# In the second block's mixer, the delta rule's steps and the taps of its q and v are traced ahead of the linear attention's

## The chip, the cores and the metric

The kernel runs on one core of one Trainium2 chip. The core has a matrix engine (PE, whose weight loads are listed apart as PEld), a vector engine (DVE), an activation engine (ACT), GpSimd (POOL), and a queue engine (SP) that issues the loads from memory. Each engine takes its instructions in a fixed order, one after the other, and an instruction starts when the work it depends on is done. The metric is the device time of one execution in microseconds (us).

## What is computed

Two transformer blocks of 256 tokens, one after the other; each has a sequence mixer and a feed-forward part. The change touches the second block's mixer of the 256 "latent" tokens. It multiplies the normalized tokens by one weight matrix of 1024 x 4624 and splits the product into the inputs of two mixers of four heads with 128 channels each, whose outputs are gated, normalized by head, put side by side and multiplied by an output matrix. Of the reference:

```python
def gla_chunk_scan(q, k, v, log_f, s0):        # the linear attention ("hg")
    '''S_t = diag(f_t) S_{t-1} + k_t v_t^T, o_t = S_t^T q_t.'''

def gated_delta_chunk_scan(q, k, v, beta, log_a, s0):   # the delta rule ("dn")
    '''S_t = a_t (I - beta_t k_t k_t^T) S_{t-1} + beta_t k_t v_t^T, o_t = S_t^T q_t.'''
    ...
    sol = lax.linalg.triangular_solve(a_mat, rhs, left_side=True, lower=True, unit_diagonal=True)

def gated_head_norm(o, gate, w):
    y = rms_norm_2(o, w) * jax.nn.silu(gate)

def hybrid_mixer_2(pc, px, lb, hg_norm_w, conv_w, a_log, dt_bias, dn_norm_w):
    ...
    return jnp.concatenate([hg_c, dn_c], axis=-1), jnp.concatenate([hg_x, dn_x], axis=-1)
```

Both recurrences run in both directions. The delta rule's q, k and v go through a 3 x 3 convolution first. After the mixer come the output projection with its residual, a router, and 16 experts.

## The kernel before

**The mixer of the latents** (`mixer2`, L1585 to L1631) is a row of projections with side work between them. For every 1 MB tile of weights, `wtile` (L260) starts a load, `split_to` (L242) makes the high part of it on ACT (a CAST) and the low part on DVE (`whl`, L243), and three products of high and low parts go to the PE (L223, tile `b`). After every tile, `pump` (L200) steps the side work: a list of Python generators, `side`, of which it takes the first, steps it once, and puts it at the back; one that returns "idle" (it waits for data that is not there yet) is passed over. `rate` says how many steps a tile gets, 5 at first and 6 later. `drain` steps on until the list is empty.

**The side generators** are:
- `dn_conv` (L1254): a projection of the delta rule (k, then q, then v), and a generator `taps` with the eight shifted products of the convolution on DVE (`qkv`, L1282).
- `dn_core` (L1318): the delta rule for two blocks of 128 tokens in two directions. The triangular inverse is built up in levels: on the PE `qp` and `dy`, on ACT a copy `Q` (L1429), on DVE a masked copy into `Y` (L1436) and transposes `T` (L1418). Then come the attention matrices (`qk`, `rb`, `att`), the weights `wT`, and four steps one after the other (`vn`, `qs`, `dno`, `su`; the last addition to the output `o` is at L1547), and at the end the head norm with the buffer `hnq`.
- `hg_core` (L1167): the linear attention in eight levels, 0 to 7. A level has four exponentials on ACT into `qq` and `kk` (L1200 to L1203), a product on DVE (`qq`, L1204), 16 matrix instructions (`hs`), two masked copies on DVE (`at`, L1210; in the last level two copies into `U` on ACT), and four operations on POOL that prepare the next level's exponents (`U` and `A`, L1213 to L1216). After the last level: two exponentials and two products of `A` (L1219, L1220), then the outputs (`ho`) and the head norms with the buffer `kk`.
- `head_norm` (L1234): for each of two blocks of tokens, four squares on ACT with a sum (L1238), a power on POOL (`hns`), four scaled copies on ACT (L1246), a product on DVE (L1247), four transposes on the PE (L1250), and a split into `l_hi` and `l_lo`, which the output projection reads. Its 96 products of 512 columns are `b<-whl,l_hi` and `b<-whl,l_lo`.

**What sets the order.** All of this runs under a scheduler (L2091) that takes the program in the order in which it was traced, weighs it with a timeline of its own, and fixes the order on each engine. So the order in which `pump` steps the generators decides the engines' order, but not alone.

Of the kernel before, what the change touches and what calls it, by code (L numbers as in the profile page):

```python
# [141 lines left out]
def tile_model(ctx: ExitStack, tc: tile.TileContext, aps: dict, out: bass.AP, dbg=None):  # L142
# [51 lines left out]
    side = []  # L194
    rate = [1]

    def pool(name):

        return tc.tile_pool(name=name, bufs=1, side="right" if tagsel[0] == "F" else "left")

    def pump(n=1, only=None):
        todo = side if only is None else only
        for _ in range(n):
            if not todo or tagsel[0] != "A":
                return
            tagsel[0] = "F"
            for _ in range(len(todo)):
                g = todo.pop(0)
                try:
                    r = next(g)  # L210
                    todo.append(g)
                    if r != "idle":
                        break
                except StopIteration:
                    break
            tagsel[0] = "A"

    def drain():
# [79 lines left out]
    def run(g):  # L298
        try:
            while True:  # L300
                next(g)
        except StopIteration as e:
            return e.value
# [96 lines left out]
    def norm_mod(*args, **kw):  # L400
        run(norm_steps(*args, **kw))
# [710 lines left out]
    def hg_tiles(hp):  # L1112
        def big(n):
            return hp.tile([P, 4, 256], F32, name=n)

        A, U = [[big(f"{n}{d}") for d in range(2)] for n in "AU"]
        v = [hp.tile([P, 512], F32, name=f"hv{b}") for b in range(2)]
        g = [hp.tile([P, 4, P], F32, name=f"hg{b}") for b in range(2)]
        return A, U, big("hq"), v, g
# [175 lines left out]
    def dn_gates(hi, lo, res, dp, hp):  # L1295

        wh = hp.tile([P, KT * 16], F32R, name="abh")
        wl = hp.tile([P, KT * 16], F32R, name="abl")
        split_to(wh, wl, col("abw"))
        o = bank("abT")  # L1300
        for k in range(KT):
            mm3(o[:16, :256], (wh[:, k * 16:(k + 1) * 16], wl[:, k * 16:(k + 1) * 16]),
                (hi[:, k, :], lo[:, k, :]), k == 0, k == KT - 1)
        abT = dp.tile([16, 256], F32, name="abT")
        nc.scalar.copy(abT, o[:16, :256])
        res["ab"] = abT
# [276 lines left out]
    def mixer2(Shg, Sdn, a, sh):  # L1583
        w = aps["w_in_2"]
        with tc.tile_pool(name="m2", bufs=1) as mp, ExitStack() as right:  # L1585
            dp = right.enter_context(tc.tile_pool(name="m2d", bufs=1, side="right"))
            zg = [dp.tile([P, 4, P], F32, name=f"zg{b}") for b in range(2)]
            hi = mp.tile([P, KT, 256], F32R, name="l_hi")
            lo = mp.tile([P, KT, 256], F32R, name="l_lo")
            norm_mod(a, sh, hi, lo)  # L1590
            res = {}
            with tc.tile_pool(name="hgr", bufs=1) as rp:
                hv = rp
                NS = 2
                raw = hg_tiles(rp)
                taps = run(dn_conv(1, hi, lo, True, res, dp, hv, NS))
                dn_gates(hi, lo, res, dp, hv)
                dn = dn_core(res, Sdn, True, dp, True)
                side.extend([taps, dn])
                rate[0] = 5  # L1600
                run(hg_raw(hi, lo, raw, 0))
                run(hg_raw(hi, lo, raw, 1))
                run(taps)
                gates = hg_gates(raw, hv, NS)
                side.append(gates)
                run(hg_raw(hi, lo, raw, 2))
                run(gates)
                rate[0] = 6
                side.append(hg_core(*raw, Shg, hi, lo, res))
                qt = run(dn_conv(0, hi, lo, True, res, dp, hv, NS))  # L1610
                side.append(qt)
                run(hg_rest(hi, lo, raw, 0))
                run(qt)
                vt = run(dn_conv(2, hi, lo, True, res, dp, hv, NS))
                side.append(vt)
                run(hg_rest(hi, lo, raw, 1))
                po = run(proj_tok(w, 4096, hi, lo))
                for b, o in enumerate(po):
                    nc.scalar.activation(flat(zg[b]), o, AF.Silu)
                    nc.gpsimd.tensor_mul(zg[b], zg[b], row("dnn").unsqueeze(1).to_broadcast([P, 4, P]))  # L1620

                res["zg"] = zg
                res["done"] = hi, lo
                drain()
            dump("d_mh", f32(hi).rearrange("p k t -> p (k t)"))
            dump("d_ml", f32(lo).rearrange("p k t -> p (k t)"))
            right.close()
            states.close()
            if stop != "mx2":
                wload.extend(wloader(moes.enter_context(tc.tile_pool(name="mw", bufs=1, side="right"))))  # L1630
                wload[1](NMW)  # L1631
            out_proj(aps["w_out_2"], hi, lo, MOD["g1_2"], after=after)
# [471 lines left out]
```

## Time and profile before

| | us |
|---|---|
| median of three runs (1550.26 to 1551.28) | 1550.29 |
| the profiled execution | 1556.02 |
| its span in the trace | 1554.2 |

The profiled execution is 5.7 us above the median, and 1.8 us of it lie around the span. PE is busy for 1407.8 us of the span (91%), DVE for 955.1, ACT for 634.8, POOL for 157.3. The latents' mixer has its projections up to 1136.5 us after the span's start; the delta rule's attention starts at 1169.5, its last output is complete at 1211.5, and the experts take the stretch from about 1250 to 1540.

In the rows below, a timeline row gives the start, the duration, the engine, the line, the operation and `out<-in`; xN says that N instructions in a row are put together. In square brackets stands the idle time of the engine before it and what ended it. A row of windows gives the length of a stretch, the busy time and the number of instructions of each engine, and PEclk, the share of the full clock that the PE was granted.

### The profile page before, as it was taken

The page shows a single profiled execution, that of the slowest core. Times are in us where ns is not written, and L with a number is a line of the kernel's source. Part 1 is how long each engine was busy: PE and PEld are TensorE (multiplying, and loading weights), DVE is VectorE, ACT ScalarE, POOL GpSimd, SP SyncE. Part 2 cuts the span into 40 slices and gives each one's busy share as a digit, 9 for nine tenths or more (in the row PEclk, how much of TensorE's full clock was granted, in tenths as well). Part 3 has the DMA queues.
Part 4 walks back from the last instruction along what each step waited for, and adds up shares of the span by engine and source line. Part 5 has one row for each costly group of instructions (what it writes and reads, how often), then busy time and mean ns, then how long its engine had stood idle before and what let it go on. Part 6 is the DMA issues. An engine that isn't in the chain of part 4 may idle for free. (4 is left out here: it accounts for less than half of the span.)

```text
span 1554.2 us, 20809 instructions
## 1 busy us (share of the span) xinstructions
PE 1407.8 (91%) x8039; PEld 1061.2 (68%) x8039; DVE 955.1 (61%) x1526; ACT 634.8 (41%) x1020; POOL 157.3 (10%) x213
## 2 busy tenths in 40 slices
PE   4988698999999999999999997988899897989996
PEld 2666445677787798997788886888797753444442
DVE  1577869786888977755455566799944532223232
ACT  2643234554555435344444444864641411111211
POOL 2013220000001000001000000134402100000000
PEclk9997798999999999999999997999897978999998
DMA  9444558787789842443355552323210696999990
GB/s 353 161 152 139 200 209 307 245 293 260 268 279 328 299 154 96 136 136 130 128 189 189 180 182 94 128 83 108 82 55 1 229 340 227 362 358 388 393 355 29
DMA packets 133471, 320.35 MB, mean 206 GB/s; under 512 B 6632, under 2 KB 25064, under 8 KB 124112
## 3 DMA queue, kind: packets, MB, share of 16 engines
q1 hardware_dynamic: 130848, 311.31, 56.8%
q0 software_dynamic: 2480, 7.16, 1.3%
q8 instruction: 86, 1.41, 0.4%
q14 instruction: 57, 0.47, 0.1%
HBM read 317.37 MB, written 1.07 MB: 205 GB/s over the span
## 5 line engine op out<-in xcount | busy, mean ns | idle before, releaser
L243 DVE TENSOR_TENSOR whl<-raw,whl 128x1024 fp32r<-128x1024 f32 x252 | 311.1, 1242 | 179.2 <-ACT whl L243 178.7
L243 ACT CAST whl<-raw 128x1024 fp32r<-128x1024 f32 x252 | 261.8, 1047 | 320.2 <-PE b L223 115.3
L223 PE MATMUL gu<-whl,f_hi 128*128 128x512 f32 (+1 forms) x768 | 230.4, 383 | 1.8 <-DVE whl L243 1.8
L223 PEld LDWEIGHTS gu<-whl,f_hi 128*128 128x128 f32 x768 | 139.6, 189 | 34.7 <-DVE whl L243 3.4
L223 PE MATMUL gu<-whl,f_lo 128*128 128x512 f32 (+1 forms) x384 | 144.3, 377 | 0.0
L333 DVE SCALAR_TENSOR_TENSOR gva<-raw,csil,gva 128x1024 f32<-128x1024 f32 x98 | 123.4, 1291 | 16.9 <-DMA raw<-in_ada_w_dram 16.7
L223 PE MATMUL do<-whl,th 128*128 128x512 f32 x352 | 114.0, 400 | 0.3 <-DVE whl L243 0.2
L223 PE MATMUL gu<-mw,xg 128*64 128x512 f32 x384 | 91.7, 629 | 13.4 <-PEq L1964 11.2
L223 PEld LDWEIGHTS gu<-whl,f_lo 128*128 128x128 f32 x384 | 72.6, 189 | 14.2 <-issue 0.5
L223 PE MATMUL b<-l_hi,whl 128*128 128x256 f32 x384 | 75.4, 296 | 5.5 <-DVE whl L243 5.5
L223 PEld LDWEIGHTS gu<-mw,xg 128*64 128x64 f32 x384 | 32.7, 144 | 69.7 <-issue 65.7
L223 PEld LDWEIGHTS do<-whl,th 128*128 128x128 f32 x352 | 65.8, 188 | 17.0 <-DVE whl L243 1.8
L223 PE MATMUL b<-s_hi,whl 128*128 128x256 f32 x384 | 73.3, 287 | 0.0
L223 PE MATMUL do<-whl,tl 128*128 128x512 f32 x176 | 69.1, 396 | 0.0
L223 PEld LDWEIGHTS b<-l_hi,whl 128*128 128x128 f32 x384 | 61.9, 196 | 8.4 <-DVE whl L243 5.9
L223 PEld LDWEIGHTS b<-s_hi,whl 128*128 128x128 f32 x384 | 60.4, 189 | 0.7 <-issue 0.7
L223 PE MATMUL b<-whl,l_hi 128*128 128x512 f32 x160 | 52.8, 409 | 5.5 <-DVE whl L243 4.1
L1930 DVE SCALAR_TENSOR_TENSOR yf<-dn,gs,gbc 64x512 f32<-64x512 f32 (+1 forms) x36 | 25.9, 720 | 51.8 <-PEq L1964 47.7
L1282 DVE SCALAR_TENSOR_TENSOR qkv<-raw,cols_sb,qkv 128x189 f32<-128x189 f32 (+3 forms) x112 | 56.6, 551 | 0.0
L1891 DVE TENSOR_TENSOR sl<-sl,gu 128x256 f32<-128x256 f32 (+1 forms) x17 | 7.0, 413 | 79.4 <-ACT sl L1890 79.4
L223 PE MATMUL b<-l_lo,whl 128*128 128x256 f32 x192 | 55.6, 290 | 0.0
L223 PE MATMUL b<-s_lo,whl 128*128 128x256 f32 x192 | 54.9, 286 | 0.0
(549 smaller groups left out, 2723.6 us busy)
## 6 DMA issues: line engine op xcount, KB each, us to landing
raw<-in_ada_w_dram SPq DMA_DIRECT2D x48, 1024.0 KB, 5.1
raw<-in_w_in_dram SPq DMA_DIRECT2D x28, 1024.0 KB, 4.9
raw<-in_w_mod_dram SPq DMA_DIRECT2D x24, 1024.0 KB, 5.0
mw<-in_w_gate_dram SPq DMA_DIRECT2D x48, 512.0 KB, 12.2
mw<-in_w_up_dram SPq DMA_DIRECT2D x48, 512.0 KB, 11.5
raw<-in_ffn_w_gate_dram SPq DMA_DIRECT2D x22, 1024.0 KB, 5.1
raw<-in_ffn_w_up_dram SPq DMA_DIRECT2D x22, 1024.0 KB, 5.0
mw<-in_w_down_dram SPq DMA_DIRECT2D x22, 1024.0 KB, 11.9
```

Source lines behind the costliest of these rows:

```text
L223: return nc.tensor.matmul(o, l, r, start=start, stop=stop)
L243: return nc.scalar.copy(hi, src), nc.vector.tensor_sub(lo, src, f32(hi))
L333: nc.vector.scalar_tensor_tensor(acc[:, c], raw[:, c], csil[cn][:, kt, 0:1], acc[:, c], op0=ALU.mult, op1=ALU.add)
L1282: nc.vector.scalar_tensor_tensor(yy, ov[:, r0 + dr:r1 + dr, c0 + dc:c1 + dc], c[:, 3 * a + b:3 * a + b + 1], yy, op0=ALU.mult, op1=ALU.add)
L1891: s2 = nc.vector.tensor_mul(sl[:, :c], sl[:, :c], o[:, c:2 * c])
L1930: nc.vector.scalar_tensor_tensor(yv, o[v, :c], gs[v, :], g2[v, n * c:(n + 1) * c], op0=ALU.mult, op1=ALU.mult)
```

## The change

A list `urgent` is added. A generator in it keeps its place at the head of the side work: `pump` steps it again and again until it returns "idle", and only then the others. The delta rule is put in the list, then the taps of its q and those of its v. The linear attention is not in it.

```diff
@@ pump @@
                     r = next(g)
-                    todo.append(g)
+                    if g in urgent and r != "idle":
+                        todo.insert(0, g)
+                    else:
+                        todo.append(g)
                     if r != "idle":
                         break
...
+            for g in reversed(urgent):
+                if g in todo:
+                    todo.remove(g)
+                    todo.insert(0, g)
@@ mixer2 @@
                 dn = dn_core(res, Sdn, True, dp, True)
+                urgent.append(dn)
                 side.extend([taps, dn])
...
                 qt = run(dn_conv(0, hi, lo, True, res, dp, hv, NS))
+                urgent.append(qt)
                 side.append(qt)
...
                 vt = run(dn_conv(2, hi, lo, True, res, dp, hv, NS))
+                urgent.append(vt)
                 side.append(vt)
```

No instruction is added or taken away; the engines' orders change, from about the 16th weight split of this mixer to its end. In the rows of after, the lines are 9 higher (L223 is L232, L243 is L252, L1204 is L1213, L1210 is L1219, L1220 is L1229, L1238 is L1247, L1246 is L1255, L1250 is L1259, L1282 is L1291, L1418 is L1427, L1436 is L1445).

On DVE, about the last weight splits of the projections (`whl`), before, starting with the product `qq` of the linear attention's last level:

```order
L1204 TENSOR_TENSOR qq<-qq,hq 128x1024
L1282 SCALAR_TENSOR_TENSOR qkv_9094<-raw,cols_sb,qkv_9094 128x3x63
L243 TENSOR_TENSOR whl<-raw,whl 128x1024
L1282 SCALAR_TENSOR_TENSOR qkv_9094<-raw,cols_sb,qkv_9094 128x192
L1220 TENSOR_TENSOR A_7467<-A_7467,hq 128x1024
L1282 SCALAR_TENSOR_TENSOR qkv_9094<-raw,cols_sb,qkv_9094 128x192
L1220 TENSOR_TENSOR A_7466<-A_7466,hq 128x1024
L243 TENSOR_TENSOR whl<-raw,whl 128x1024
L1282 SCALAR_TENSOR_TENSOR qkv_9094<-raw,cols_sb,qkv_9094 128x3x63 x2
L243 TENSOR_TENSOR whl<-raw,whl 128x1024
L1436 COPY_PREDICATED Y_7893<-cst_72,dy 128x32x8
```

and after, starting with the `qq` of level 5:

```order
L1213 TENSOR_TENSOR qq<-qq,hq 128x1024
L252 TENSOR_TENSOR whl<-raw,whl 128x1024 x2
L1219 COPY_PREDICATED at_8831<-cst_72,hs 128x512
L1219 COPY_PREDICATED at_8832<-cst_72,hs 128x512
L1445 COPY_PREDICATED Y_7893<-cst_72,dy 128x32x8
L1213 TENSOR_TENSOR qq<-qq,hq 128x1024
L1427 STREAM_TRANSPOSE T<-Y_7893 128x512
L1445 COPY_PREDICATED Y_7903<-cst_72,dy 128x32x8
L1445 COPY_PREDICATED Y_7974<-cst_72,dy 128x32x8
L1427 STREAM_TRANSPOSE T<-Y_7903 128x512
```

The 32nd and the 33rd split of the projections' weights stand right behind level 5 now; the products of levels 6 and 7 and of `A` come behind them. Before, all eight levels and `A` came ahead of the 33rd. Counted up to that split, DVE has three `qq`, six `at` and two transposes `T` fewer in front, and one tap more; POOL has about 11 of its operations fewer there.

On the PE, from the last products of the projections (`b<-whl`) on, before:

```order
L223 MATMUL b<-whl,l_hi 128x512 x2
L223 MATMUL b<-whl,l_lo 128x512
L223 MATMUL ho<-hv_7470,at_8266 128x128
L223 MATMUL ho<-hv_7471,U_7468 128x128
L223 MATMUL ho<-Shg,A_7466 128x128
L223 MATMUL ho<-Shg,A_7467 128x128
```

and after:

```order
L232 MATMUL b<-whl,l_hi 128x512 x2
L232 MATMUL b<-whl,l_lo 128x512
L232 MATMUL dy<-Y_7974,Q 128x64 x4
L232 MATMUL hs<-qq,kk 128x128 x8
L232 MATMUL dy<-Y_7984,Q 128x64 x4
L232 MATMUL qp<-T,a 128x64 x16
L232 MATMUL dy<-Y_7893,Q 128x64 x4
L232 MATMUL hs<-qq,kk 128x128 x8
L232 MATMUL dy<-Y_7903,Q 128x64 x4
L232 MATMUL dy<-Y_7974,Q 128x64 x4
L232 MATMUL ho<-hv_7470,at_8831 128x128
```

The `hs` of levels 6 and 7 stand behind the projections now, with the delta rule's level 4 (`qp`, `dy`) between them. (One row of the PE here is two instructions in the trace, save for the products of weights.)

On ACT, at the end of the mixer, before:

```order
L243 CAST l_hi<-b 128x4x128
L1238 ACTIVATE kk,hns<-ho 128x128 x4
L1246 ACTIVATE kk<-ho,hns 128x128 x4
L1238 ACTIVATE hnq,hns<-o 128x128 x8
L243 CAST l_hi<-b 128x4x128
L1246 ACTIVATE hnq<-o,hns 128x128 x4
L243 CAST whl<-raw 128x1024
L1246 ACTIVATE hnq<-o,hns 128x128 x4
```

and after:

```order
L1247 ACTIVATE hnq,hns<-o 128x128 x8
L1255 ACTIVATE hnq<-o,hns 128x128 x4
L1247 ACTIVATE kk,hns<-ho 128x128 x4
L1255 ACTIVATE hnq<-o,hns 128x128 x4
L252 CAST l_hi<-b 128x4x128
L1255 ACTIVATE kk<-ho,hns 128x128 x4
L252 CAST l_hi<-b 128x4x128 x2
L1247 ACTIVATE kk,hns<-ho 128x128 x4
L1255 ACTIVATE kk<-ho,hns 128x128 x4
L252 CAST l_hi<-b 128x4x128
```

Before, the linear attention's head norm (`kk`) of the first block is long done at that place and that of the second stands ahead of the delta rule's (`hnq`); after, both stand behind the squares of `hnq`. On the PE the same is to be seen: after the last `dno`, eight transposes of `hnq` and four of `kk` come ahead of the first 18 products of the output projection, and four more of `kk` ahead of the other 78. Before, 24 of the 96 stood ahead of the transposes of `hnq`.

## Rows read from the trace of the kernel before

**Rows 1.** Windows: us, busy (instructions) by engine, PEclk, DMA share, GB/s.

```profile
1040.00:1110.00 70.00, 62.20 (x415) 56.05 (x414) 69.01 (x97) 38.49 (x62) 28.03 (x21) 0.98 0.28 98
1110.00:1120.00 10.00, 8.74 (x36) 8.27 (x37) 10.00 (x18) 1.16 (x3) 2.34 (x2) 0.55 0.19 54
1120.00:1136.50 16.50, 15.91 (x92) 13.84 (x92) 15.19 (x23) 15.40 (x20) 2.17 (x2) 0.96 0.35 116
1136.50:1169.50 33.00, 32.83 (x289) 32.11 (x288) 12.26 (x21) 11.09 (x32) 3.71 (x4) 1.00 0.08 30
1169.50:1211.50 42.00, 38.68 (x236) 30.89 (x236) 20.05 (x41) 8.12 (x22) 10.55 (x10) 0.80 0.00 1
1250.00:1540.00 290.00, 263.13 (x1500) 127.10 (x1499) 82.70 (x195) 53.95 (x111) 1.15 (x2) 0.96 0.84 316
```

**Rows 2.** Timeline of DVE about 1075: the same operations alone and beside POOL.

```profile
1070.20 1.21 DVE L1204 TENSOR_TENSOR qq<-qq,hq 128x1024 f32<-128x1024 f32 x1
1071.34 0.69 DVE L1418 STREAM_TRANSPOSE T<-Y 128x512 f32<-128x512 f32 x1
...
1073.04 1.21 DVE L243 TENSOR_TENSOR whl<-raw,whl 128x1024 fp32r<-128x1024 f32 x1
...
1074.70 0.38 DVE L1282 SCALAR_TENSOR_TENSOR qkv<-raw,cols_sb,qkv 128x189 f32<-128x189 f32 x1
...
1075.53 3.64 DVE L1282 SCALAR_TENSOR_TENSOR qkv<-raw,cols_sb,qkv 128x189 f32<-128x189 f32 x3
1079.09 2.13 DVE L243 TENSOR_TENSOR whl<-raw,whl 128x1024 fp32r<-128x1024 f32 x1
1081.15 0.73 DVE L1210 COPY_PREDICATED at<-cst,hs 128x512 f32<-128x512 uint32 x1
```

**Rows 3.** Timeline of POOL then: first and last of one level's four operations.

```profile
1075.48 1.11 POOL L1213 TENSOR_TENSOR U<-U,A 128x512 f32<-128x512 f32 x1 [7.09 <-ACT kk L1202]
...
1078.91 1.23 POOL L1216 TENSOR_TENSOR A<-A 128x512 f32<-128x512 f32 x1
```

**Rows 4.** Timeline of PE: a wait, and `qp` and `hs` after it.

```profile
1111.26 0.80 PE L223 MATMUL b<-whl,l_hi 128*128 128x512 f32 x1 [2.41 <-DVE whl L243]
...
1113.56 3.51 PE L223 MATMUL qp<-T,a 128*128 128x64 f32 x16
1116.86 3.73 PE L223 MATMUL hs<-qq,kk 128*128 128x128 f32 x16
...
1126.11 1.89 PE L223 MATMUL qp<-T,a 128*128 128x64 f32 x16
```

**Rows 5.** Timeline of ACT: a table load and one of four exponentials.

```profile
1120.65 1.28 ACT L1200 ACT_TABLE_LOAD   x1 [3.18 <-DVE T L1418]
1121.95 0.63 ACT L1200 ACTIVATE qq<-A 128x512 f32<-128x512 f32 x1
```

**Rows 6.** Timeline of ACT at the end of the mixer: the head norms.

```profile
1208.40 0.28 ACT L1238 ACTIVATE kk<-ho 128x128 f32<-128x128 f32 x1
...
1210.95 1.14 ACT L1246 ACTIVATE kk<-ho,hns 128x128 f32<-128x128 f32 x4 [1.40 <-POOL hns L283]
1211.96 0.33 ACT L1238 ACTIVATE hnq<-o 128x128 f32<-128x128 f32 x1
...
1214.30 0.58 ACT L243 CAST l_hi<-b 128x512 fp32r<-128x512 f32 x1
1216.82 1.28 ACT L1246 ACTIVATE hnq<-o,hns 128x128 f32<-128x128 f32 x4 [1.94 <-POOL hns L1244]
```

**Rows 7.** Timeline of DVE: the delta rule's last output.

```profile
1210.78 0.69 DVE L1547 TENSOR_TENSOR o<-o,dno 128x512 f32<-128x512 f32 x1 [0.23 <-PE dno L223]
```

**Rows 8.** Timeline of PE: the output projection's products.

```profile
1214.93 0.74 PE L223 MATMUL b<-whl,l_hi 128*128 128x512 f32 x2 [1.41 <-ACT l_hi L243]
...
1221.47 1.88 PE L223 MATMUL b<-whl,l_hi 128*128 128x512 f32 x7
...
1239.79 0.39 PE L223 MATMUL b<-whl,l_lo 128*128 128x512 f32 x1
```

More of the change, by code (lines that the diff above doesn't have):

```diff
@@ L195, in tile_model @@
     rate = [1]
+    urgent = []
     def pool(name):
```

## The prediction

> **What bounds the kernel now.** I read the windows first, then the timeline of the engine that is full in them. From 1040 to 1136.5 us, in the second half of the projections, DVE is the bound: busy for 69.0 of 70 us, then for all of 10, then for 15.2 of 16.5, while the PE has 7.8, 1.3 and 0.6 us idle [rows 1]. The longest of these ends with the low part of a weight (2.41 us, at 1111.26) [rows 4]: DVE is late with `whl`, because taps, masked copies and products of both mixers stand in its queue. From 1136.5 to 1169.5 the PE is the bound, busy for 32.8 of 33 us at full clock. The 42 us after that are the delta rule's dependent chain, and the experts from 1250 to 1540 are the PE's again, 263 of 290 us [rows 1]. A shift of the mixer's end therefore reaches the kernel's end one to one.
>
> **What the change moves.** The orders show that it doesn't do quite what its words say. Counted in projection products, `qp` and `dy` of the delta rule don't come earlier; what happens is that the linear attention comes later. Levels 6 and 7 and the products of `A`, which stood among the projections, stand behind them, and its head norms stand behind the delta rule's.
>
> **The front: what DVE is relieved of.** Ahead of the 33rd weight split there are three `qq` fewer at 1.21 us, six `at` at 0.73, two `T` at 0.69, and one tap more at 0.38 [rows 2]: 3.6 + 4.4 + 1.4 - 0.4 = 9.0 us. About 11 operations of POOL leave the stretch too, and these slow DVE: three taps took 3.64 us where three alone take 1.14, and the next `whl` 2.13 against 1.21 [rows 2], beside the four operations of one level [rows 3]. That is 2.5 + 0.9 = 3.4 us for four, 0.86 each, and 11 x 0.86 = 9.4 us. In sum DVE is relieved of 18.4 us.
>
> The Trainium skill ("SBUF — State Buffer", Who interferes with whom) says that a DVE instruction with two SBUF inputs and a GpSimd instruction that reads SBUF exclude each other for the whole length of whichever started first. The trace agrees that taps and splits suffer, but shows 0.86 us for each operation of POOL, not its whole 1.1 to 1.2 us; by the rule's whole length the relief would be an estimated 22 us instead of 18.4, which the next paragraph caps in any case.
>
> **What the PE can make of it.** The work of the PE ahead of the attention is the same, so the gain at 1169.5 is at most the idle time that goes, 7.8 + 1.3 + 0.6 = 9.7 us, and the slow clock that goes: from 1110 to 1120, behind the wait of 2.41 us, the granted clock was 0.55 [rows 1, 4], that is nearly the lower of the two levels, 1.2 of 2.4 GHz; `qp` took 3.51 us there and 1.89 later, `hs` 3.73 [rows 4]. Busy for 8.7 us at 0.55 is 4.8 at full clock, so 3.9 us are to be had. The ceiling is 13.6 us, less than DVE's 18.4. Below it, two engines that hand on work in fixed orders always lose something: in the one stretch of the front in which DVE wasn't full, 1120 to 1136.5, the PE still idled for 3.6% [rows 1]; of the 83 us that would be left this is 3 us. I let half of the slow clock go, since one wait can bring it back. That makes 9.7 - 3 + 2 = 8.7 us, bounds 0 (the PE finds something else to wait for) and 13.6; I take the value between, as the stretch that it is taken from is the nearest.
>
> **Does the late linear attention become the new wait?** Its chain from the exponentials of level 5 on: POOL's four operations 4.7 us [rows 3]; level 6 with a table load of 1.28 and four exponentials of 0.63, overlapped to about 2.2 [rows 5], 3.5; POOL again 4.7; level 7 3.5; two operations of POOL 2.3; an exponential of `A` at twice 0.63 less its overhead, about 1.1, and a product of 1.2 [rows 2]. In sum 21 us until `ho` can start. In that time the PE has, by its order: the wait for the split that follows `qq` (1.4 + 1.2 us), 24 products of the projections at some 0.25 us each [rows 8], 5.9, three `hs` of about 1.9 (half of the slow 3.73), and in `qp` and `dy` four to five times 1.9 [rows 4]: 22 to 24 us. The chain is just hidden. I put new waits at nothing, and up to 5 us if POOL or ACT come late; that is in the lower bound above.
>
> **The middle.** Attention, weights and the four steps keep their order and their 42 us [rows 1].
>
> **The end: what it costs.** T is the delta rule's last output, 1211.47 [rows 7]. Before, the linear attention's first head norm is done by then, the second in work, and 24 of the 96 products of the output projection get done ahead of T + 10.0 (1221.47); the other 72 end at T + 28.7, 18.7 us with all that lies between them [rows 8]. After, ACT has the eight squares of `hnq` first, T + 0.5 to T + 2.8 (eight from 1211.96 to 1214.30), then copies that wait for POOL, at about T + 4 to 5.4 (1.9 us and more after the squares; 1.28 long), then the squares of `kk` (1.2 us, 1208.40 to 1209.6), copies of `hnq` (1.28) and `l_hi` (0.58), and at T + 8.4 the copies of `kk` [rows 6]. From such copies to the first product that needs them it took 4.0 us before (1210.95 to 1214.93, of which some 0.7 behind squares) [rows 6, 8]; so the output projection begins at about T + 11.8. The squares for the second block stand behind the `l_hi` of the first, so at about T + 11.5, and from squares to product it took 6.5 us (1208.40 to 1214.93) [rows 6, 8], 5.8 without the queue: T + 17.6. The 78 products that are left take 78/72 of 18.7, 20.3 us, to T + 37.9 against T + 28.7: 9.2 us lost. Here the wait is new and its queue is the PE's: behind the transposes of `kk` stands the whole output projection, behind that the router and the experts.
>
> **The clock at the end.** Between T + 1 and T + 11.8 the PE has only twelve transposes. From 1169.5 to 1211.5 it was busy for 38.7 of 42 us and still had a mean clock of 0.80 [rows 1]; after ten idle microseconds it will be at the lower level. The first 18 products, some 4.6 us, then take up to 9.2 and end at T + 21.0 instead of before T + 17.6: 0 to 3.4 us, and 5 if the rest starts slow too (ten microseconds at 0.55, as after 1111 [rows 1]). I take 1.7, the middle of the first. The Trainium skill ("TensorE: Matmul & The Clock Gate", Loop structure matters more than you think) says that matmuls that each wait for their data run cold, and speaks against this change: by it all of the 18 would be slow, an estimated 3.4 instead of 1.7.
>
> **Sum.** -8.7 + 9.2 + 1.7 = +2.2 us. Against the profiled execution that is 1556.0 + 2.2 = 1558.2; that one lies 5.7 above the median, and the same shift on the median gives 1552.5, 0.14% more than 1550.29.
>
> **The rivals.**
> - Slower: the lower clock decides the end. If the PE, after its ten idle microseconds, is at the lower level beyond T + 17.6, the end costs 9.2 + 5 = 14 us; with a front that gives 5, since the clock falls in its new gaps as well, the kernel comes to +9, 1559.3. For it: the stretch at 0.55 lasted ten microseconds though the PE was busy for 8.7 of them [rows 1]. Against it: in the steps ahead of T the clock holds, and in the front the gaps get shorter.
> - Faster: the front reaches its ceiling, 13.6 us, and the end costs only its 9.2: -4.4, 1545.9. For it: DVE is relieved of more than the PE can use, and the chain of the linear attention is hidden. Against it: that chain is hidden by 2 us at most, and every hand-over has to be in time.
> - The change does nothing where it should: the delta rule is no earlier, the PE stays as idle as it is, say since each weight's high part on ACT or a product of the chain takes the place of DVE's. Then the end alone is left: +10.9, 1561.2. Against it: in the front DVE is at 98 to 100% and the wait of 2.41 us names it [rows 1, 4].
>
> **How the numbers follow.** A measurement of this kernel tells about 0.2%, 3.1 us, from no change, so "the same" is 1547.2 to 1553.4. The forecast has half of the chance: 1552.5, with an own range of 1550 to 1556 (a front of 6 to 11); of it 0.38 lie within 0.2%, 0.10 above, 0.02 below. The slower rival has 0.22, the faster 0.20, the last 0.08 (0.02 of that the same). Faster 0.22, same 0.40, slower 0.38. The range, 1546 to 1560, leaves out about 0.1 at either end: half of the faster rival, and the last with the worst of the slower.
>
> **What would show it.** In the profile after: the last product of the projections near 1123 to 1128 instead of 1136.5; `hs` of two levels behind it with no wait of more than 1 us; `qn` at about 1161 instead of 1169.5; POOL's operations beside an idle DVE there; between the last `o` and the last output product some 38 to 40 us instead of 28.7, with a PE that has two gaps, the first of about 10 us, ended by `l_hi`. The prediction is wrong if `ho` waits for `A` by more than 5 us (then the chain wasn't hidden), if the front keeps its waits for `whl`, or if the output projection starts before T + 9.

## The result and the profile after

The changed kernel takes 1569.30 us (median of four, 1564.70 to 1572.99) against 1550.78 of before on the same chip: 1.0114 times the time, 95% interval 1.0090 to 1.0139. That is slower, and 9 us beyond the upper end of the range. The profiled execution, the slowest of its four, took 1572.99 us (span 1571.1), 17 more than that of before. By stages, read from the timelines of both (M0 is the start of the first transposes of k in this mixer, ahead of everything that the change moves; T is the end of the delta rule's last output):

| stage, us | before | after | difference | forecast |
|---|---|---|---|---|
| span's start to M0 | 1000.8 | 1002.1 | +1.3 | 0 |
| M0 to the projections' last product | 135.9 | 121.6 | -14.3 | |
| from there to `qn` (the tail) | 32.8 | 44.2 | +11.3 | |
| the front, these two together | 168.7 | 165.8 | -2.9 | -8.7 |
| `qn` to T | 41.9 | 42.4 | +0.5 | 0 |
| T to the last output product | 28.7 | 40.9 | +12.2 | +10.9 |
| from there to the experts' first product | 15.2 | 14.5 | -0.6 | 0 |
| that product to the span's end | 298.8 | 305.4 | +6.6 | 0 |

The windows of after, by stage; the columns are those of [rows 1]:

```profile
1041.30:1111.30 70.00, 62.67 (x411) 55.66 (x411) 70.00 (x103) 36.76 (x58) 30.85 (x22) 0.98 0.27 92
1111.30:1123.70 12.40, 12.39 (x81) 10.80 (x79) 9.70 (x13) 11.10 (x16) 5.61 (x4) 1.00 0.25 87
1123.70:1131.00 7.30, 4.86 (x40) 4.62 (x40) 7.30 (x11) 6.56 (x10) 6.85 (x5) 1.00 0.42 144
1131.00:1143.20 12.20, 12.04 (x64) 12.05 (x65) 6.67 (x10) 5.52 (x11) 4.72 (x4) 0.58 0.01 1
1143.20:1167.90 24.70, 24.54 (x219) 24.04 (x218) 5.82 (x12) 4.47 (x12) 0.00 (x0) 1.00 0.00 1
...
1210.30:1221.70 11.40, 3.29 (x12) 2.15 (x12) 3.37 (x6) 8.76 (x40) 5.06 (x12) 0.65 0.00 0
1221.70:1228.50 6.80, 6.78 (x18) 5.30 (x19) 1.38 (x2) 2.15 (x12) 1.83 (x3) 0.59 0.11 33
1228.50:1251.20 22.70, 22.02 (x109) 17.80 (x108) 11.39 (x13) 8.45 (x13) 0.00 (x0) 1.00 0.96 361
```

Up to the projections' end at 1123.7 the PE is busy for 12.39 of 12.40 us at full clock; before, that place had the wait of 2.41 us and the clock of 0.55 [rows 1, 4]. Behind it come two stretches that weren't there: 7.3 us in which the PE stands still for 2.4 and DVE is full, then 12.2 us of a full PE at a clock of 0.58. The PE's timeline there, from the first operations behind the projections to the first `ho`:

```profile
1124.34 1.10 PE L232 MATMUL dy<-Y,Q 128*128 128x64 f32 x8 [0.65 <-DVE Y L1445]
1126.44 2.02 PE L232 MATMUL hs<-qq,kk 128*128 128x128 f32 x16 [1.00 <-ACT zg L1631]
1128.30 1.00 PE L232 MATMUL dy<-Y,Q 128*128 128x64 f32 x8
1129.14 1.06 PE L232 MATMUL qp<-T,a 128*128 128x64 f32 x8
1131.16 4.87 PE L232 MATMUL qp<-T,a 128*128 128x64 f32 x24 [0.96 <-DVE Y L1445]
1135.82 1.91 PE L232 MATMUL dy<-Y,Q 128*128 128x64 f32 x8
1137.53 3.73 PE L232 MATMUL hs<-qq,kk 128*128 128x128 f32 x16
1141.05 2.35 PE L232 MATMUL dy<-Y,Q 128*128 128x64 f32 x16
1143.23 0.44 PE L232 MATMUL ho<-hv,at 128*128 128x128 f32 x2
```

Three waits make 2.6 us, and after the third the same `hs` takes 3.73 us that took 2.02 ahead of it. So the tail's 11.3 us are: the `hs` of two levels that were moved there, 2 x 1.87 = 3.7 (half of the slow 3.73); the waits, 2.6; and the lower clock, 12.0 us for work that is 12.0 x 0.58 = 7.0 at full clock, 5.0. In sum 11.3. The first of these is work that the projections' 14.3 us have lost, not new work.

The PE at the end of the mixer:

```profile
1208.21 1.16 PE L232 MATMUL dno<-vn,att 128*128 128x128 f32 x8
1216.08 1.11 PE L1259 MATMUL b<-cst,hnq 128*128 128x128 f32 x4 [6.71 <-DVE hnq L1256]
1218.43 1.09 PE L1259 MATMUL b<-cst,hnq 128*128 128x128 f32 x4 [1.24 <-DVE hnq L1256]
1219.95 1.09 PE L1259 MATMUL b<-cst,kk 128*128 128x128 f32 x4 [0.43 <-DVE kk L1256]
1221.72 1.22 PE L232 MATMUL b<-whl,l_hi 128*128 128x512 f32 x2 [0.68 <-ACT l_hi L252]
...
1228.55 0.60 PE L1259 MATMUL b<-cst,kk 128*128 128x128 f32 x4
1229.82 0.74 PE L232 MATMUL b<-whl,l_hi 128*128 128x512 f32 x2 [0.68 <-ACT l_hi L252]
```

T is 1210.28, so the first product comes at T + 11.4. The 18 products of the first block take 6.8 us at a clock of 0.59, where 18 of 0.23 each, the spacing of these products at full clock, would be 4.1; the second block's transposes, whose `kk` DVE finished at 1225.98, stand behind them until 1228.55, and the other 78 products begin at T + 19.5.

Of the experts' 6.6 us, 4.7 have one place, the third expert; they are lost by the start of the row below. The other 1.9 lie behind it and aren't explained: among the kernels without the wait described here this stretch is 295.0 to 298.9 us long. The PE's wait in after, and what DVE's sequencer does there (instructions of the expert's branch, with first and last start):

```profile
1330.23 5.08 PE L232 MATMUL gu<-mw,xg 128*64 128x512 f32 x16 [6.79 <-DVEq L1976]
```

```profile
L1976 DVEq EVENT_SEMAPHORE  x2: 21/21/21, 1330.0 to 1330.1; - x2
L1976 DVEq ALU_OP  x1: 40/40/40, 1324.4 to 1324.4; - x1
L1976 DVEq COMPARE_BRANCH  x1: 80/80/80, 1324.5 to 1324.5; - x1
```

and the same two views of before:

```profile
1315.19 5.35 PE L223 MATMUL gu<-mw,xg 128*64 128x512 f32 x16 [2.03 <-ACTq L1964]
```

```profile
L1964 DVEq EVENT_SEMAPHORE  x2: 21/21/21, 1314.8 to 1315.0; - x2
L1964 DVEq ALU_OP  x1: 47/47/47, 1314.1 to 1314.1; - x1
L1964 DVEq COMPARE_BRANCH  x1: 92/92/92, 1314.2 to 1314.2; - x1
```

Between its branch and its next instruction DVE passes 0.6 us before and 5.4 us after. It has no operation in that time, and the trace names no other engine that it waits for. Ahead of the first expert's branch DVE has executed 1596 instructions before and 1601 after; the five more are waits on semaphores that the other order needs, so the change does add instructions, though none that computes.

### The profile page after: what moved, and what is told of

The parts are those of the page before. It is cut to its first block, busy times and chain, and to the rows that moved or that the text cites. A ratio compares the mean times of both kernels' runs of the same rounds, so it can differ in the third digit from the quotient of the medians.

```text
span 1571.1 us, 20814 instructions
## 1 busy us (share of the span) xinstructions
PE 1415.4 (90%) x8039; PEld 1066.6 (68%) x8039; DVE 951.4 (61%) x1526; ACT 636.1 (40%) x1020; POOL 158.2 (10%) x213
## 5 line engine op out<-in xcount | busy, mean ns | idle before, releaser
L252 DVE TENSOR_TENSOR whl<-raw,whl 128x1024 fp32r<-128x1024 f32 x252 | 311.9, 1244 | 175.8 <-ACT whl L252 175.2
L252 ACT CAST whl<-raw 128x1024 fp32r<-128x1024 f32 x252 | 262.1, 1047 | 317.4 <-PE b L232 117.7
L232 PE MATMUL gu<-whl,f_hi 128*128 128x512 f32 (+1 forms) x768 | 229.5, 381 | 1.9 <-DVE whl L252 1.9
L232 PEld LDWEIGHTS gu<-whl,f_hi 128*128 128x128 f32 x768 | 138.8, 188 | 34.3 <-issue 4.3
L232 PE MATMUL gu<-whl,f_lo 128*128 128x512 f32 (+1 forms) x384 | 143.8, 376 | 0.0
L232 PE MATMUL do<-whl,th 128*128 128x512 f32 x352 | 113.7, 400 | 0.2 <-ACT whl L252 0.2
L232 PE MATMUL gu<-mw,xg 128*64 128x512 f32 x384 | 92.9, 636 | 18.2 <-PEq L1976 10.9
L232 PEld LDWEIGHTS gu<-mw,xg 128*64 128x64 f32 x384 | 33.1, 146 | 75.3 <-issue 74.2
L232 PEld LDWEIGHTS gu<-whl,f_lo 128*128 128x128 f32 x384 | 72.2, 188 | 14.3 <-issue 0.7
L232 PEld LDWEIGHTS do<-whl,th 128*128 128x128 f32 x352 | 65.7, 188 | 16.6 <-DVE whl L252 1.3
L232 PE MATMUL b<-s_hi,whl 128*128 128x256 f32 x384 | 73.3, 287 | 0.0
L232 PE MATMUL b<-l_hi,whl 128*128 128x256 f32 x384 | 73.0, 289 | 0.1
L232 PE MATMUL do<-whl,tl 128*128 128x512 f32 x176 | 69.1, 396 | 0.0
L232 PEld LDWEIGHTS b<-l_hi,whl 128*128 128x128 f32 x384 | 60.5, 190 | 2.3 <-issue 1.9
L232 PEld LDWEIGHTS b<-s_hi,whl 128*128 128x128 f32 x384 | 60.4, 189 | 0.7 <-issue 0.7
L1291 DVE SCALAR_TENSOR_TENSOR qkv<-raw,cols_sb,qkv 128x189 f32<-128x189 f32 (+3 forms) x112 | 57.4, 562 | 0.0
L232 PE MATMUL b<-whl,l_hi 128*128 128x512 f32 x160 | 55.4, 417 | 1.4 <-ACT l_hi L252 1.4
L232 PE MATMUL b<-s_lo,whl 128*128 128x256 f32 x192 | 54.9, 286 | 0.0
L232 PE MATMUL b<-l_lo,whl 128*128 128x256 f32 x192 | 54.4, 284 | 0.0
```

Source lines behind the costliest of these rows:

```text
L232: return nc.tensor.matmul(o, l, r, start=start, stop=stop)
L252: return nc.scalar.copy(hi, src), nc.vector.tensor_sub(lo, src, f32(hi))
L1291: nc.vector.scalar_tensor_tensor(yy, ov[:, r0 + dr:r1 + dr, c0 + dc:c1 + dc], c[:, 3 * a + b:3 * a + b + 1], yy, op0=ALU.mult, op1=ALU.add)
```

## The experiments

Theory: the mixer's end costs some 11 us, the front gives little because the linear attention's chain and the clock take back what the projections gain, and the experts' 6.6 us come from the place of DVE's code, not from the mixer. Rivals: the end's cost needs the new front, the chain isn't what takes the front's gain, and the experts lose by the new order itself. Two parts of the theory as it first stood were not borne out: that filling the PE's gap gives some of the end back (e4), and that POOL's two products for the gate `zg` make the chain late (e8). The stages of all profiled executions, in the manner of the first table, with the time for which DVE stands still behind its branch in the third expert ("still stand"). There is one such execution of each kernel, so a row shows what that execution did and not how it spreads:

| kernel | projections | tail | front | `qn` to T | T to last product | experts to the end | still stand |
|---|---|---|---|---|---|---|---|
| before | 135.9 | 32.8 | 168.7 | 41.9 | 28.7 | 298.8 | no |
| after | 121.6 | 44.2 | 165.8 | 42.4 | 40.9 | 305.4 | 5.4 |
| e1, end alone | 135.8 | 32.8 | 168.6 | 37.3 | 40.4 | 295.0 | no |
| e2, norms first, before | 134.3 | 32.8 | 167.1 | 48.7 | 22.5 | 298.0 | no |
| e3, norms first, after | 121.7 | 44.2 | 165.9 | 49.5 | 22.8 | 302.3 | 5.2 |
| e4, gap filled | 121.5 | 40.0 | 161.5 | 37.0 | 40.7 | 301.7 | 3.9 |
| e5, before and 5 memsets | 135.9 | 32.8 | 168.8 | 42.0 | 28.7 | 301.5 | 5.3 |
| e6, after and 24 memsets | 120.9 | 40.1 | 161.0 | 37.1 | 40.9 | 295.0 | no |
| e7, delta rule alone urgent | 127.5 | 41.6 | 169.1 | 37.5 | 40.1 | 297.1 | no |
| e8, gate on DVE | 121.6 | 44.4 | 166.0 | 37.3 | 40.4 | 298.2 | no |
| e9, before and 24 memsets | 137.4 | 32.8 | 170.2 | 36.7 | 28.7 | 298.9 | no |
| e10, norms first, 24 memsets | 121.7 | 40.2 | 161.9 | 48.7 | 22.2 | 297.4 | no |

**The end alone, on the front of before.** The delta rule says when its head norms are done, and the linear attention waits for it ahead of its last products:

```diff
@@ dn_core @@
+            res["dn"] = 1
@@ hg_core @@
+            while "dn" not in res:
+                yield "idle"
```

> The kernel before, with one thing of the change: the linear attention's outputs and head norms are traced behind the delta rule's (its output stage waits for a mark that the delta rule sets at its end). The projections keep the order of before. Theory (the late head norms are the main cost): the delta rule's last output stays at about 1211.5 us, the output projection's last product comes 11 to 13 us later than the 1240 of before, and the kernel takes 1562 to 1569 us, since the experts add some us to any delay. Rival (the loss comes from the changed order among the projections and in the tail): the kernel stays within 3 us of before, 1547 to 1554.

Measured: 1560.25 (1558.83 to 1567.22), 1.0077 [1.0049, 1.0106]: +9.3 us. T to the last product is 40.4 us with the front of before, so the end's cost needs nothing of the new front. The time is below the 1562 to 1569 that was expected: the experts add nothing to the delay here, they take 295.0 us. Its rows on the PE have the durations of after:

```profile
1213.52 1.12 PE L1252 MATMUL b<-cst,hnq 128*128 128x128 f32 x4 [6.71 <-DVE hnq L1249]
...
1219.16 1.22 PE L223 MATMUL b<-whl,l_hi 128*128 128x512 f32 x2 [0.68 <-ACT l_hi L243]
```

**The other way about: the linear attention's norms first.** Attention and delta rule wait until the linear attention has its head norms and its 48 of the 96 output products, once on the kernel before and once on the changed one:

```diff
@@ hg_core, at its end @@
+            res["hg"] = 1
@@ ahead of the attention @@
+                if lat and both:
+                    yield from wait("hg")
```

> The kernel before, but the delta rule waits with its attention until the linear attention's head norms are traced, so that they, and 48 products of the output projection that need nothing else, stand among the attention's instructions. Theory (what costs is what stands behind the delta rule's last output): from that output to the last product 21 to 23 us instead of 28.7, while the attention gets longer by some 3 to 8 us (48 products are 11 us, the PE idles and runs slowly there); kernel 1546 to 1553 us. Rival (the products only move and the attention gets longer by all of the 11 us): 1553 to 1556 us.

> The changed kernel with the same wait: the delta rule's attention is traced behind the linear attention's head norms; the projections keep the changed order. Theory (of the 18.5 us the end has 12 and the experts the rest; the front gives 1 to 2): 1544 to 1553 us, within 3 us of the run of before with the same wait. Rival (the changed order among the projections or the jitter of the experts belongs to the front): 8 us and more above that run, with the experts' stretch longer than the 299 us of before.

Measured: 1558.44 (1.0051 [1.0032, 1.0070]) and 1562.65 (1.0081 [1.0064, 1.0098]). T to the last product falls to 22.5 and 22.8 us, but `qn` to T grows to 48.7 and 49.5, since the 48 products now stand in the delta rule's chain. From M0 the mixer's last product comes after 238.4 and 238.2 us, against 239.4 in before: the repair only levels the mixer. Both times lie above what was expected of them. That e3 is 4.2 us slower than e2 agrees with the experts, where DVE stands for 5.2 us; e10 below puts it to the test. Why e2 takes 7.5 us more than before isn't settled: its profiled execution is only 2.4 above that of before, and it reaches M0 4.2 later.

**The gap at the end filled.** After, with 28 dead matmuls behind the delta rule's last product, so that the PE has no gap of ten microseconds:

```diff
+                        if step == 1 and dr == 1:
+                            w = bank("su")
+                            for i in range(28):
+                                h = i % 4
+                                mm(w[:, h * P:(h + 1) * P], AT[c, dr][:, h, :], vn[:, h, :])
```

> The changed kernel with 28 matrix products more behind the delta rule's last dno, whose result nobody reads: some 6 us of work in the gap of 6.7 us on the PE. Theory (the lower clock after the gap costs 2 to 3 us): the first 18 products of the output projection take 4.2 to 4.6 us instead of 6.8, the last transposes of kk start 2 to 3 us earlier against the delta rule's last output, and the last product comes 37 to 39 us after it instead of 40.9. Rival (the clock costs nothing, the chain of head norms sets the time): it stays at 40 to 41.5 us.

Measured: 1563.99 (1.0075 [1.0051, 1.0099]), and 40.7 us from T to the last product: nothing gained at the end, as the rival had it and not the theory. Its windows, from the dead products on:

```profile
1206.40:1211.40 5.00, 5.00 (x47) 5.00 (x47) 0.12 (x1) 3.67 (x20) 3.01 (x9) 1.00 0.00 0
1211.40:1217.00 5.60, 2.78 (x21) 1.96 (x19) 3.28 (x5) 4.62 (x20) 2.03 (x4) 0.98 0.00 0
1217.00:1225.00 8.00, 7.52 (x22) 5.83 (x22) 1.38 (x2) 2.60 (x13) 1.83 (x3) 0.58 0.18 65
```

While the dead products ran the clock was full, and the transposes behind them took 0.63 us instead of 1.1. But the transposes wait for DVE and ACT as before; the PE was busy for 2.78 of 5.6 us among them, and then the clock fell, to 0.58, for just the 18 products. So these products cost what they cost in after, and whether the end would be shorter with the clock held through them stays open.

**The place of the code.** A few one-element memsets on DVE in the kernel's set-up (dead work) move all of DVE's later instructions; in the traces every engine's operations keep their order but for them. Five went into the kernel before, 24 into the changed one, 24 into the one before, and 24 into e3's.

```diff
+    for _ in range(5):
+        nc.vector.memset(cp.tile([P, 1], F32, name="pad"), 0.0)
```

> The kernel before with five DVE instructions more at its start (memsets of 128 numbers that nobody reads); the rest keeps its order. In the changed kernel DVE has five instructions more ahead of the experts' branches than before (1601 to 1596), and stands still for 3.9 to 5.4 us behind one branch of the third expert; in kernels without the five it doesn't. Theory (what the experts lose is a matter of where DVE's code lies, not of the mixer's order): a gap of 4 to 5.5 us on DVE behind a branch of the third expert, from the first expert's first product to the end 301 to 305 us instead of 295 to 299, kernel 3 to 6 us slower, 1554 to 1557 us. Rival (the gap comes from loads that collide since the mixer ends later): no such gap, no change in the time.

> The changed kernel with 24 such DVE instructions more at its start. Theory (place of the code): the gap on DVE at the third expert is gone or at another branch; where it is gone, the experts take 295 to 300 us and the kernel 1559 to 1565 us. Rival (the later end of the mixer makes the gap): it stays, 1565 to 1573 us.

> The kernel before with 24 one-element memsets on VectorE in its set-up (dead work, about 2 us at most, beside the loads of the start). It is the control of the changed kernel with the same 24 memsets (1562.1 us). Theory 1 (place of the code plus order of the mixer): 24 more instructions put VectorE's first expert branch at about the 1620th instruction, away from the 1600th and 1601st where VectorE stood still for 3.9 to 5.4 us; so the time stays within 4 us of before (1547 to 1555), first expert product to the end takes 295 to 300 us, the mixer's end T to last product 28 to 29 us, and what is left between this kernel and the changed kernel with the memsets, 8 to 14 us, is the mixer's order. Rival: it is the padding itself, wherever it puts the branch (then 5 memsets, 1560.1 us, did what any padding does): 1557 to 1564 us, and the order of the mixer costs nothing when the padding is equal.

> The changed kernel, in which the linear attention's head norms and their 48 output products are traced ahead of the attention (as in the run without memsets, 1562.7 us), with the 24 memsets. It takes both named costs away: the longer end and the place of the code. Theory 1: T to last product 22 to 24 us, the mixer's end as in before (238 to 239 us after its first transposes), no still stand of VectorE in the third expert, first expert product to the end 295 to 300 us, so 1549 to 1556 us in all, level with before. Rival (the front's order costs in its own right, by the lower clock of the tail or by what it does to the experts): 1558 us or more with the experts' stretch over 300 us and no still stand of VectorE in it.

Measured: with five, the kernel before takes 1560.14 (1.0059 [1.0038, 1.0079]), with 24 it takes 1553.95 against 1553.09 (0.9999 [0.9974, 1.0023]). After with 24 takes 1562.14 (1.0079 [1.0052, 1.0105]) instead of 1569.30, and e3's with 24 takes 1556.22 (1.0009 [0.9991, 1.0026]) instead of 1562.65. Five memsets thus cost the kernel before 8.6 us, or 9.2 by the ratio: more than the 1554 to 1557 that was expected, and more than a still stand of 5.3 us. The profiled execution doesn't show where the rest lies; it has 2.7 us more than before in the experts, and 7.2 ahead of M0. In the kernel before, five memsets bring the very rows of after, and in after 24 take them away; the PE's wait and DVE's branch in e5, then in e6:

```profile
1324.12 6.41 PE L223 MATMUL gu<-mw,xg 128*64 128x512 f32 x16 [6.71 <-DVEq L1966]
```

```profile
L1966 DVEq EVENT_SEMAPHORE  x2: 21/21/21, 1323.9 to 1324.0; - x2
L1966 DVEq ALU_OP  x1: 40/40/40, 1318.4 to 1318.4; - x1
L1966 DVEq COMPARE_BRANCH  x1: 80/80/80, 1318.5 to 1318.5; - x1
```

```profile
1319.46 5.35 PE L232 MATMUL gu<-mw,xg 128*64 128x512 f32 x16 [2.04 <-ACTq L1978]
```

```profile
L1978 DVEq EVENT_SEMAPHORE  x2: 21/21/21, 1319.1 to 1319.2; - x2
L1978 DVEq ALU_OP  x1: 40/40/40, 1318.4 to 1318.4; - x1
L1978 DVEq COMPARE_BRANCH  x1: 80/80/80, 1318.5 to 1318.5; - x1
```

Over all twelve kernels the still stand is there where DVE has executed 1600 or 1601 instructions ahead of its first expert branch (after, e3, e4, e5) and not where it has executed 1595 or 1596 (before, e1, e2, e7) or 1603 and more (e8, e6, e9, e10). So it goes by how many instructions stand ahead, that is by the place of the code, and the mixer's order brought it on only by its waits. The rival, that padding costs in its own right, falls with e9. With the place of the code out of the way on both sides, the change costs 1562.14 against 1553.95, 8.2 us, or 12.4 by the ratios (1.0079 less 0.9999, since the two ran on different chips; the two intervals together leave an estimated 7 to 18): that is what the new order costs without the still stand. The two profiled executions don't show all of it in the mixer. From M0 to the mixer's last product e6 takes 239.0 us and e9 235.6, 3.4 less; e6 also comes to M0 8.1 us later, where all twelve kernels have had the same order on every engine but for the memsets, and is 3.9 shorter in the experts. e10 takes both named costs away and is level with before.

**Which part of the front gives and which takes.** The delta rule alone urgent, the taps not; and after with the gate's product on DVE instead of POOL, in which it stands between the products of level 6:

```diff
@@ mixer2, for e7 @@
-                urgent.append(qt)
...
-                urgent.append(vt)
@@ mixer2, for e8 @@
-                    nc.gpsimd.tensor_mul(zg[b], zg[b], row("dnn").unsqueeze(1).to_broadcast([P, 4, P]))
+                    nc.vector.tensor_mul(zg[b], zg[b], row("dnn").unsqueeze(1).to_broadcast([P, 4, P]))
```

> The changed kernel with the delta rule alone in the list of urgent generators, not the taps of q and v. One level of the linear attention instead of two then stands behind the last projection. Theory (the gain of the front is lost in the tail because the linear attention's last levels are late: ACT's activations of the taps and POOL's products of the gate stand ahead of them, and the PE waits and falls to the lower clock): the last projection at 1125 to 1131, the attention's start (qn) at 1161 to 1166 instead of 1167.9, the end as in the changed kernel (39 to 41 us from the delta rule's last output to the last product). Rival (the tail is as long whatever the order, since its work is the same): qn at 1167 to 1171.

> The changed kernel with the two products of the delta rule's gate (zg, 1.27 us each) on DVE instead of POOL, where they stand between the operations of the last levels. Theory (POOL's chain from level 5 to the outputs, 26.8 us instead of the 21 that were forecast, makes the tail long): from the end of level 5's exponentials to the first ho 22 to 25 us, and qn 2 to 4 us earlier against the last projection (40 to 42 us instead of 44.2). Rival (the PE's own order and clock set the tail): 43.5 to 45 us.

Measured: e7 1564.61 (1.0082 [1.0050, 1.0113]). Its projections end 8.4 us earlier than before's, its tail is 8.8 longer, and `qn` is 0.4 later: with the delta rule alone ahead there is no gain of the front at all; the theory had expected one, with `qn` at 1161 to 1166 (it came at 1175.5, with M0 5.6 us later than in before). The other 6 us at the projections' end come with the urgent taps. Its PE behind the projections:

```profile
1136.50 3.51 PE L232 MATMUL hs<-qq,kk 128*128 128x128 f32 x16 [2.58 <-DVE qq L1213]
...
1144.57 0.80 PE L232 MATMUL ho<-hv,at 128*128 128x128 f32 x2 [2.83 <-ACT U L1216]
```

Here `hs` and `ho` wait for the linear attention by name, for DVE's `qq` and ACT's `U`. e8, of which there is one run, 1562.09 us, has a tail of 44.4 us as after has, and in place of the wait for the gate another:

```profile
1135.55 3.67 PE L232 MATMUL qp<-T,a 128*128 128x64 f32 x16 [2.13 <-ACT Q L1438]
```

So taking POOL's two products away didn't shorten the tail here. The test isn't a clean one: the scheduler changed more than the gate's place (on ACT the exponentials of the last level now begin with `qq` instead of `kk`, on the PE a `qp` went ahead of the last `hs`), the clock was at 0.62 in the first 7.3 us behind the projections and at 0.72 in the next 12.2, and tails of one and the same order differ by 4 us with the clock (e6 and after). So a gain of some microseconds isn't ruled out. Why e8's experts lost nothing agrees with the place of the code (1603).

## Why the prediction was wrong

Three steps of the prediction failed: the new waits of the front put at nothing, the clock's term there, and the shift of the mixer's end that was to reach the kernel's end one to one. Between the forecast of +2.2 and the +17 of the two profiled executions lie about 15 us: the front with 5.8, the end with 1.3, the experts with 6.6, the stretch ahead of M0 with 1.3, the rest with less than 1. None of the three signs that the prediction named for being wrong was seen: `ho` doesn't wait for `A`, the waits for `whl` are gone, and the output projection starts after T + 9.

**The front's first half was right.** "The last product of the projections near 1123 to 1128": it ends at 1123.7. The PE's waits for `whl`, four with 9.6 us between M0 and the projections' end before, are gone, and so is the clock of 0.55, as forecast. DVE is busy for 111.6 us between M0 and the projections' end instead of 125.4, so it is relieved of 13.7 us, where 18.4 were worked out; that was still enough.

**"The chain is just hidden" failed, with "new waits at nothing".** The chain from the end of level 5's exponentials (1116.39) to the first `ho` (1143.23) is 26.8 us instead of 21. POOL's rows show most of the rest:

```profile
1124.15 1.06 POOL L1222 TENSOR_TENSOR U<-U,A 128x512 f32<-128x512 f32 x1 [2.54 <-ACT kk L1211]
1125.17 2.04 POOL L1223 TENSOR_TENSOR U<-U,A 128x512 f32<-128x512 f32 x1
1127.18 1.27 POOL L1632 TENSOR_TENSOR zg<-zg,rows_sb 128x512 f32<-128x512 f32 x1
1128.41 2.04 POOL L1224 TENSOR_TENSOR A<-A 128x512 f32<-128x512 f32 x1
1130.41 1.27 POOL L1632 TENSOR_TENSOR zg<-zg,rows_sb 128x512 f32<-128x512 f32 x1
1131.64 1.06 POOL L1225 TENSOR_TENSOR A<-A 128x512 f32<-128x512 f32 x1
```

Level 6 takes 8.5 us on POOL, 1124.15 to 1132.70, where 4.7 were put in: two of its operations take twice their time beside a DVE that is full until 1131.0, and two products of the gate, which had been overlooked, stand in between. Taking the gate away alone doesn't shorten the tail of e8: the PE then waits for the delta rule's `Q`, and after 1131 the PE itself is what is late. The prediction had the contention with POOL slow DVE and forgot that it slows POOL as well.

**The clock's term had the wrong size and place.** Half of 3.9 us was to come back. It all did, at 1111 to 1124 (1.00), and 5.0 were lost anew at 1131 to 1143 (0.58), behind 2.4 us of stillness in 7.3. In e4 and e6 the tail is 4 us shorter with the same order: the clock is low in the first 7 us behind the projections, in which the PE had waits in after, and full from then on. In the first stretch the PE then waits for little, since it is itself the late one. The windows of e6's tail:

```profile
1130.10:1137.50 7.40, 7.07 (x41) 7.01 (x41) 7.08 (x11) 5.02 (x7) 7.40 (x6) 0.62 0.39 139
1137.50:1149.70 12.20, 11.45 (x103) 11.31 (x102) 8.02 (x11) 6.33 (x12) 4.19 (x4) 1.00 0.00 1
```

"The gaps get shorter", said against the slower rival, held for the projections and not for what stands behind them. Against the 168.7 us of before, the front is -2.9 in after and -2.8 in e3, where the low clock comes late (0.58 behind 7.3 us at 1.00), and -7.2, -7.7 and -6.8 in e4, e6 and e10, where it comes first. These five have the same order on the PE to the end of the tail, and on the other engines beyond the first `ho`. So the profiled execution of after is of the unlucky kind, and with the other kind the forecast of -8.7 would have been near. What decides between the two isn't shown.

**The middle was right as a difference, with a spread that the prediction lacked.** `qn` to T takes about 42 us or about 37 with the same order: 42.0 in e5 and 36.7 in e9, which are both the kernel before, and 42.4 in after and 37.1 in e6. So the +0.5 of the first pair is a draw. The clock differs between the two kinds:

```profile
1171.40:1208.10 36.70, 32.23 (x236) 27.53 (x236) 21.17 (x41) 8.10 (x22) 10.84 (x10) 1.00 0.00 1
```

This is e9, at 1.00; before had 0.80 there [rows 1], so that "in the steps ahead of T the clock holds" was no argument against the slower rival. Ahead of M0 the executions differ by up to 8.5 us too (1000.8 in before, 1009.3 in e6), with the same order on all engines but for the memsets. Whole spans of single executions therefore say little; medians say more, and stages show where.

**The end was right in mechanism and near in size**: +12.2 against +10.9, with the first product at T + 11.4 (T + 11.8) and the whole projection queued behind the transposes. The longest gap ahead of it is 6.7 us, and `hnq` ends it; `l_hi` ends the last, of 0.7. The second block starts at T + 19.5, where the forecast with its clock term had 17.6 + 1.7 = T + 19.3 (its own terms, 11.5 + 5.8, give 17.3 for the 17.6). Most of the missing 1.3 us is in the 78 products behind it, which take 21.4 us instead of 20.3. The 18 products lost 2.7 us by the clock. The Trainium skill ("TensorE: Matmul & The Clock Gate", Loop structure matters more than you think) says that matmuls that each wait for their data run cold, which the prediction worked out as 3.4 us beside the 1.7 that it took. The trace agrees in kind: the first three transposes, each behind a wait, took 1.1 us here. But behind the dead products of e4 they took 0.63, though two of them waited there too.

**The slower rival was the nearest for the mixer, in part by luck.** It had a front of 5 and an end of 14, +9; the mixer of the first pair came to -2.9 + 0.5 + 12.2 = +9.8. The lower level of the clock in the front's new gaps, which it names, is seen there. Its end isn't: the clock was low up to T + 18.2, where the 18 products end, and 1.00 behind that. And e6 against e9 has +3.4 for the mixer, nearer to the forecast, though medians of the two are 8 to 12 apart.

**"A shift of the mixer's end therefore reaches the kernel's end one to one" failed.** The experts took 6.6 us more, most of it DVE's still stand, which no term and no rival had; without it (e6) the time is 1562.1, still above the range. This was not to be seen in any duration; the number of DVE's instructions ahead of the branches, 1596 and 1601, was to be had from the two programs, but not what it does.

## What to carry over

When a queue is relieved to let one chain pass, follow the chain that is put behind it to its first consumer, with every instruction that stands between on all engines and with contention counted for both sides; what was hidden among long work is no longer hidden behind it, and the same order can then cost 4 us more or less with the clock. At the end of a stage, work that needs no late input belongs ahead of the late input, but only as much of it as the late chain leaves idle (e2, e3). And before an order is called slower by less than a per cent in a program with branches, shift the code by a few instructions on both sides and time again.

## What the runs showed of the hardware

Behind one and the same branch DVE stood still for 3.9 to 5.4 us or for 0.6, by the number of instructions ahead of it: five semaphore waits (after) or five memsets (e5) brought the still stand on, and 24 memsets took it away (e6, e10). The Trainium skill ("Runtime: NRT & Kernel Launch", Instruction fetch mechanics) says that a taken branch whose target lies outside the two blocks of instructions that an engine holds makes it wait for a load of that block; that would do what is seen here. The trace shows blocks of instructions loaded at that place in kernels with the still stand and without, so it doesn't show that this is the cause. It speaks for it that in all four kernels with the still stand DVE goes on 0.4 to 1.2 us after the second of two such loads of 8 KB (in after they end at 1328.31 and 1328.97, and DVE goes on at 1330.00), and that in e4, where these loads end earliest after the branch, the still stand is the shortest.

The PE's clock fell to 0.58 after stretches in which the PE was busy for 4.86 of 7.30 us (after, 1123.7 to 1131) and for 2.78 of 5.60 (e4), and stayed there through 12.2 and 8 us in which it was nearly full. The 6.5 us of dense dead work right ahead of the second of them didn't prevent it.

The same work in the same order took 4 to 5 us more or less in different executions, with the clock low at other times or not at all: the tail 44.2 or 40.1 us (after, e6), `qn` to T 42.0 or 36.7 (e5, e9).
